# A down projection done once as seven block products instead of once per group

## Chip, cores and metric

The kernel runs on one core of a Trainium2 chip, in float32. The metric is the device time of one execution in microseconds (us), the median of the runs shown. A float32 value is carried as a pair: a high part in the format that TensorE takes (`fp32r`) and a low part, the remainder. A product of two such pairs takes three matmuls (high·high, high·low, low·high), which `mm3` issues; making the pair ("split") takes one copy on ACT (the high part) and one subtraction on DVE (the low part).

## What is computed

One layer over 1024 tokens of width 1024: a half-step feed-forward, a mixer of convolution and state space, a second half-step feed-forward, a final norm. The change lies in the second feed-forward, whose inner width is 2816 (22 tiles of 128).

```python
def swiglu(h, w_gate, w_up, w_down):
    return (jax.nn.silu(h @ w_gate) * (h @ w_up)) @ w_down
...
h = modulate(rms_norm(x, ffn2_norm[l]), sh3, sc3)
x = x + 0.5 * g3[:, None, :] * swiglu(h, ffn2_w_gate[l], ffn2_w_up[l], ffn2_w_down[l])
return rms_norm(x, final_norm)
```

## The kernel before

Everything is transposed: features lie on partitions and tokens along a row, in two halves of 512 (`h` is 0 or 1). `x[k][h]` is tile k of the residual. The Python program is written in one order, and a scheduler then sets each engine's order; each engine runs its own list strictly in order. DMAs are all issued by SP, in the order of its list.

The feed-forward works in eleven groups of two inner tiles (`fi` 0 and 1). Group 0 (`group0`, tiles named `fb0`) takes the gate and up projections tile by tile with `proj`, eight `mm3` for each tile and half of the tokens. Groups 1 to 10 (`seven`, tiles `fb1` to `fb10`) take each of the two projections as a 2 by 2 block product by a scheme of seven block products instead of eight: left operands are blocks of the normalised input (`A11`, `A12`, `A22` and the sums `S1` to `S4`, made once by `combos` and named `h3S`), right operands are blocks of the weights and their sums, which POOL makes in `Weights.combine` (lines 158 to 160) into the tile `sums`. One side, gate or up, is 7 products of 4 `mm3`, so a group is 14 x 12 = 168 matmuls. They accumulate in three PSUM banks per side, of the pool `mm_ps` with six.

After a group's products, `down2` multiplies its two activation tiles with its rows of the down weights: 8 output tiles, 2 halves and 2 inner tiles make 32 `mm3`, 96 matmuls of 512 columns, and DVE adds each of the 16 results to `x` (scaled by `gate`). This is called from `between` inside the next group's `seven`, behind the product number `place`: 0 in group 1, which puts `fb0d` between the first and the second product of `fb1`, and 1 in the others. The last two groups' down projections are done together behind group 10 (`fb10d`, a loop at the end of the kernel), the last quarter of it in two pieces of 256 columns; `after2` squares each finished `x` tile for the final norm, and `Sumsq.rstd` sends the sums (`n4..st`), the root on DVE and the spreading (`n4..bc`) to PE and DVE some `mm3` later.

Weights come through `Weights`: a source array of 1 MB is loaded into one of two buffers of `rawp` (`raw`), in `granules` of two chunks of 512 columns it is split by ACT and DVE into a tile `w`, and `w` has three slots here (`ringp`), each free again when PE has done with it. A granule of `seven` serves two products, 24 matmuls. The split activations live in the pool `movA` (20 tiles of 4 KB per partition) and `movB` (12), `x` in a pool of its own.

In the profile's names, `x` tiles are `x`, split activations of a group `fb_0a` and `fb_1a`, the final norm's `n4_0_0` appears as `n_0`. Line 101 is the helper that issues the instructions of PE, ACT, DVE and SP.

Of the kernel before, what the change touches and what calls it, by code (L numbers as in the profile page):

```python
# [34 lines left out]
SEVEN_FROM = (6, 1)  # L35
J = S // TAU
# [74 lines left out]
class Weights:  # L111
# [56 lines left out]
    def pump(self):  # L168
        while self.slots and len(self.tiles) < len(self.granules):
            i = len(self.tiles)  # L170
            pair = self.granules[i]
            (j0, c0), (j1, c1) = pair
# [9 lines left out]
            if j0 == j1 and isinstance(c0, int) and c1 == c0 + 1:  # L182
# [34 lines left out]
def hymba_layer(ctx: ExitStack, tc, x_d, wm1_d, wmod_d, gu1_d, gs1_d, wd1_d, win_d, wout_d, glu_d, gu2_d, gs2_d, wd2_d, cols_d, cond_d, lam_d, bc_d, out_d):  # L217
# [13 lines left out]
    xp = pool("xp", side="right")  # L231
# [3 lines left out]
    movs = {"A": pool("movA", bufs=20)}  # L235
# [57 lines left out]
    stream(gu2_d, gs2_d, wd2_d, SEVEN_FROM[1])  # L293
# [219 lines left out]
    def seven(name, between, place=1):  # L513

        a_tiles, gate_, taken = {}, {}, []
        for side in "gu":
# [5 lines left out]
            def out(h, fi, t):  # L522
                nm = f"{name}_{fi}_{h}"
# [3 lines left out]
                else:  # L527
                    V.tensor_tensor(out=t[:], in0=t[:], in1=gate_[h, fi][:], op=ALU.mult)
                    a_tiles[fi, h] = split_act(t[:], nm + "a")

            for n, (left, b) in enumerate(SEVEN):
# [39 lines left out]
                if side == "g" and n == place:  # L571
                    between()
        return a_tiles

    def down2(a_tiles, n, name, halves=(1, 0)):
        wd = ws.take(2)
        for dh in range(2):
# [7 lines left out]
            ws.free()  # L585

# [716 lines left out]
    movs["B"] = ctx.enter_context(tc.tile_pool(name="movB", bufs=12))  # L1303
# [14 lines left out]
    ctx.callback(sums_open.close)  # L1318

    def group0():  # L1320

        a_tiles, pg, pu = {}, {}, {}
        g0, u0, g1 = ws.take(3)
        ready(act3, 0, KT)
        pg[0, 0], pu[0, 0] = proj(g0, act3[0], "fb0g0_0"), proj(u0, act3[0], "fb0u0_0")
        gu_evac(0, 0, pg[0, 0], pu[0, 0], a_tiles, "fb0_0_0")
        pg[1, 0] = proj(g1, act3[0], "fb0g1_0")
        ready(act3, 1, KT)
        pg[0, 1] = proj(g0, act3[1], "fb0g0_1")
# [7 lines left out]
        for h in range(2):  # L1337
            gu_evac(1, h, pg[1, h], proj(u1, act3[h], f"fb0u1_{h}"), a_tiles, f"fb0_1_{h}")
        ws.free()
        return a_tiles  # L1340

    clock.side.append(combos(act3, "h3", "BAAA"))
    a_prev = group0()
    blocks["free"] = True
    a_prev = seven("fb1", lambda: down2(a_prev, 2, "fb0", (0, 1)), 0)
    for g in range(2, NGRP - 1):
        a_prev = seven(f"fb{g}", lambda: down2(a_prev, 2, f"fb{g - 1}"))
    a_last, a_prev = a_prev, seven("fb10", lambda: None)
    n4 = {}
    WHOLE = [slice(0, HALF)]  # L1350
    PIECES = (WHOLE, [slice(0, HALF // 2), slice(HALF // 2, HALF)])

    def after2(d, h, tok):
        n = tok.stop - tok.start
        if d == 0:
            n4[h, tok.start] = Sumsq(f"n4_{h}_{tok.start}", n, acc_in_mov)
        ss = n4[h, tok.start]
        ss.add(x[d][h][:, tok], apart=d == KT - 1, beside=d < 6)

        def use(bc):  # L1360
            for k in range(KT):
                xs = x[k][h][:, tok]
# [88 lines left out]
```

## Time and profile before

| | |
|---|---|
| runs | 1801.97, 1801.79, 1800.12 us; median 1801.79 |
| profiled execution, span from first to last instruction | 1799.7 us |
| around the span (the three runs less the span) | 0.4 to 2.3 us; 2.1 for the median |
| matmuls, as the profile counts them | 7772 |
| busy shares | PE 96%, DVE 67%, ACT 27%, POOL 12% |
| granted TensorE clock | 0.989 of full |
| moved by DMA | 165 MB, 92 GB/s over the span |

The profile lists one execution, by its span; the time of that execution itself is not listed, so that it is taken as the span and the 2.1 us that the median lies above it. Busy time of PE counts a matmul to the end of its pipeline: the mean of one is 389 ns where one starts every 227 ns. Rates are therefore taken from starts. In the list of waits and in the timeline, what stands behind an arrow is what released the instruction.

The second feed-forward runs from 1105 us to the end.

### The profile page before, as it was taken

Reading aid. Unit: us, or ns where it says so; the run is one execution under the profiler, and the core shown is the slowest. Engines: PE = TensorE matmul, PEld = TensorE weight load, DVE = VectorE, ACT = ScalarE, POOL = GpSimd, SP = SyncE. Lnnn points to the kernel's source line nnn. Section 1 sums busy time; section 2 is a strip of 40 time slices with the busy share of each in tenths; the row PEclk is TensorE's granted clock in tenths of the full one; section 3 lists DMA queues with packets and bytes.
Section 4 is the critical chain, followed back from the end, with each engine's and each line's share of the span. In section 5 each row is a group of like instructions: output and inputs, shape, how many; then the busy total and the mean of one; then the engine's idle time right before and its main releaser. Section 6 shows DMA issues by size and latency. Waiting matters only on the chain.

```text
span 1799.7 us, 20080 instructions
## 1 busy us (share of the span) xinstructions
PE 1725.3 (96%) x7772; PEld 1421.5 (79%) x7772; DVE 1210.3 (67%) x2182; ACT 490.9 (27%) x750; POOL 222.7 (12%) x143
## 2 busy tenths in 40 slices
PE   4998989999999999999999999999999999999996
PEld 3786767788788888877888888788888888888885
DVE  7999999847765566482665737975655565556546
ACT  4311212112222223342213424432222223222331
POOL 0000000001512112110000012021212111211211
PEclk9998999999999999999999999999999999999997
DMA  7625665410111111314763110111111111111102
GB/s 305 232 72 181 208 207 203 162 48 24 47 47 50 61 54 48 111 48 119 221 200 98 48 47 24 47 48 47 62 56 47 48 65 52 47 49 66 50 24 94
DMA packets 58737, 165.02 MB, mean 92 GB/s; under 512 B 14353, under 2 KB 29969, under 8 KB 43922
## 3 DMA queue, kind: packets, MB, share of 16 engines
q1 hardware_dynamic: 58642, 163.74, 26.6%
q8 instruction: 61, 1.00, 0.2%
q14 instruction: 34, 0.28, 0.0%
HBM read 140.64 MB, written 18.87 MB: 89 GB/s over the span
## 4 chain that ended last, share of the span: by engine, by line
PE 75%; DVE 4%; DMA 1%; POOL 1%; ACT 1%; issue 0%; SPq 0%; DVEq 0%; ACTq 0%; POOLq 0%
PE wo L101 5%; PE b L101 2%; PE v L101 2%; PE c L101 2%; PE fb10d L101 2%; PE fa10d L101 2%; PE u L101 1%; PE fb0u L101 1%; PE fa5u L101 1%; PE fb8d L101 1%; PE fb7d L101 1%; PE fb6d L101 1%; PE fb5d L101 1%; PE fb4d L101 1%; PE fb3d L101 1%; PE fb2d L101 1%
## 5 line engine op out<-in xcount | busy, mean ns | idle before, releaser
L101 ACT CAST w<-raw 128x1024 fp32r<-128x1024 f32 (+1 forms) x203 | 171.6, 861 | 516.0 <-POOL raw L159 58.0
L101 DVE TENSOR_TENSOR w<-raw,w 128x1024 fp32r<-128x1024 f32 (+1 forms) x203 | 208.4, 1040 | 77.8 <-ACT w L101 75.6
L158 POOL TENSOR_TENSOR sums<-raw 128x1024 f32<-128x1024 f32 x30 | 77.5, 2582 | 1119.8 <-DVE w L101 668.8
L101 DVE TENSOR_TENSOR w<-sums,w 128x512 fp32r<-128x512 f32 x90 | 59.7, 689 | 47.0 <-ACT w L101 46.6
L101 ACT CAST w<-sums 128x512 fp32r<-128x512 f32 x90 | 52.8, 619 | 133.3 <-PE fa6d L101 9.7
L101 DVE CUSTOM_DVE_ANT_0 wm<-wm,cact 128x1024 f32<-128x1024 f32 x48 | 57.7, 1212 | 0.0
L101 PE MATMUL wo<-oa,w 128*128 128x512 f32 x192 | 45.4, 391 | 0.6 <-DVE w L101 0.6
L101 PE MATMUL u<-h,w 128*128 128x512 f32 x192 | 44.9, 392 | 0.8 <-DVE w L101 0.8
L101 PE MATMUL v<-h,w 128*128 128x512 f32 x192 | 45.4, 393 | 0.0
L101 PE MATMUL c<-h,w 128*128 128x512 f32 x192 | 45.2, 392 | 0.0
L101 PE MATMUL wo<-ob,w 128*128 128x512 f32 x192 | 45.2, 391 | 0.0
L101 PE MATMUL b<-h,w 128*128 128x512 f32 x192 | 44.9, 392 | 0.0
L101 PEld LDWEIGHTS u<-h,w 128*128 128x128 f32 x192 | 35.6, 188 | 9.1 <-DVE w L101 1.2
L101 PEld LDWEIGHTS wo<-oa,w 128*128 128x128 f32 x192 | 35.8, 188 | 8.7 <-DVE w L101 1.1
L101 PEld LDWEIGHTS wo<-ob,w 128*128 128x128 f32 x192 | 35.8, 188 | 7.4
L101 PEld LDWEIGHTS b<-h,w 128*128 128x128 f32 x192 | 35.7, 188 | 7.2
L101 PE MATMUL p<-h,w 128*128 128x512 f32 x144 | 36.1, 409 | 5.4 <-DVE h L101 3.0
L101 PEld LDWEIGHTS c<-h,w 128*128 128x128 f32 x192 | 35.6, 188 | 7.1
L101 PEld LDWEIGHTS v<-h,w 128*128 128x128 f32 x192 | 35.5, 188 | 7.0
L159 POOL TENSOR_TENSOR raw<-sums,raw 128x512 f32<-128x512 f32 x30 | 40.2, 1341 | 2.4
L160 POOL TENSOR_TENSOR sums<-raw 128x512 f32<-128x512 f32 x30 | 40.1, 1338 | 2.4
L339 POOL TENSOR_TENSOR n3aq<-n3aq,n3aq 128x512 f32<-128x512 f32 x5 | 6.5, 1291 | 267.0 <-ACT n3aq L101 266.9
(1095 smaller groups left out, 4025.1 us busy)
## 6 DMA issues: line engine op xcount, KB each, us to landing
raw<-in_gs SPq DMA_DIRECT2D x30, 1024.0 KB, 4.8
wm<-in_wmod SPq DMA_DIRECT2D x24, 1024.0 KB, 5.4
raw<-in_wd SPq DMA_DIRECT2D x22, 1024.0 KB, 4.9
raw<-in_gu SPq DMA_DIRECT2D x14, 1024.0 KB, 4.9
mw<-in_wm SPq DMA_DIRECT2D x8, 1024.0 KB, 9.3
raw<-in_win SPq DMA_DIRECT2D x8, 1024.0 KB, 5.4
x<-in_x SPq DMA_DIRECT2D x8, 512.0 KB, 7.3
mw<-in_wmod SPq DMA_DIRECT2D x4, 1024.0 KB, 4.8
```

The lines of the kernel that those rows point to most:

```text
L101: r = getattr(self.engine, name)(*args, **kw)
L158: self.G.tensor_tensor(out=f[:, :1024], in0=r[:, 512:1536], in1=r[:, :1024], op=ALU.subtract)
L159: self.G.tensor_tensor(out=r[:, 512:1024], in0=f[:, 512:1024], in1=r[:, :512], op=ALU.add)
L160: self.G.tensor_tensor(out=f[:, 1024:], in0=r[:, 1536:], in1=r[:, 512:1024], op=ALU.subtract)
L339: nc.gpsimd.tensor_tensor(out=a, in0=a, in1=sq[:, :n], op=ALU.add)
```

## The change

The activations of all eleven groups are now kept and the down projection is done once behind group 10, as a 2 by 2 block product over the whole inner width of 22 tiles (`KH` = 11 in each half).

- **Groups.** The inner tiles are ordered so that group g holds tile g of the first half and tile g of the second. `seven` and `group0` write the activations, unsplit, into two tiles of a `Left` (`fb1l` and so on). In the next group's `between`, now at place 1 in all groups and without matmuls, `Left.sums` adds four block sums on DVE (`fb1s`) and SP stores all seven left operands into DRAM (`l2_d`, 1.75 MB in seven rows of 256 KB a group). `right_sums` loads the group's 1 MB of down weights (`wd_0`, `wd_1`), makes four sums on POOL and stores them (`t2_d`); group 0's down weights are handled so in `late`, near the end of group 4, and `late` of group 10 loads and splits the first left operands of the down projection.
- **Down projection** (`down7`). Seven passes, in the order of `PASSES`; each is 11 inner tiles times 4 output tiles, 44 `mm3`. Passes write by turns into four banks X and four banks Y, so that DVE reads a pass's result while PE writes the other banks; three results are accumulated on. `Lefts` loads left operands back, two tiles of 128 by 512 at a time (`fbLr`), and splits them (`fbLh`, `fbLl`) ahead of use; the right operands come through `Weights` as granules of two chunks. The last pass goes over the tokens in two pieces of 256 columns.
- **Residual.** `x` (4 MB) is stored to DRAM in group 0 (`x2_d`) and loaded back during passes 0, 1, 2 and 4 (`y`), so that its room goes to `movA` (28 tiles). `movB` has 10 and is closed behind group 10; in its place five more slots for `w` open from pass 2 on.

PE's list at the start of `fb1` (`fb1gA<-h_0` is the first product, `h3S` are the sums; a number behind a name tells buffers apart), before:

```order
L101 MATMUL fb1gA<-h_0_8289,w_8664 128x512 x3
L101 MATMUL fb1gA<-h_0_8297,w_8664 128x512 x3
L101 MATMUL fb1gA<-h_0_8318,w_8664 128x512 x3
L101 MATMUL fb1gA<-h_0_8326,w_8664 128x512 x3
L101 MATMUL fb0d_0_8818<-fb_0_0a,w_8705 128x512 x3
L101 MATMUL fb0d_0_8818<-fb_1_0a,w_8705 128x512
L101 MATMUL fb0d_0_8826<-fb_0_0a,w_8705 128x512
L101 MATMUL fb0d_0_8818<-fb_1_0a,w_8705 128x512 x2
```

and now:

```order
L107 MATMUL fb1gA<-h_0_8289,w_8666 128x512 x3
L107 MATMUL fb1gA<-h_0_8297,w_8666 128x512 x3
L107 MATMUL fb1gA<-h_0_8318,w_8666 128x512 x3
L107 MATMUL fb1gA<-h_0_8326,w_8666 128x512 x3
L107 MATMUL fb1gB<-h3S_0_8596,w_8666 128x512 x3
L107 MATMUL fb1gB<-h3S_1_8656,w_8666 128x512 x3
L107 MATMUL fb1gB<-h3S_2_8727,w_8666 128x512 x3
L107 MATMUL fb1gA<-h_0_8334,w_8707 128x512 x2
L107 MATMUL fb1gB<-h3S_3_8785,w_8666 128x512
```

The 96 matmuls of `fb0d` stood between the first and the second product; now the second product, which reads `S2`, follows at once.

DVE's list at the same place, where the last `S2` and `S3` tiles are made (`h3S_3`), before:

```order
L101 TENSOR_TENSOR w_8795<-raw_8611,w_8795 128x1024
L101 TENSOR_TENSOR h3S_3_8785<-f_3_8765,h3S_3_8785 128x512
L101 TENSOR_TENSOR fb_1_1a<-fb_1_1af,fb_1_1a 128x512
L101 TENSOR_TENSOR h3S_3_8813<-f_3_8763,h3S_3_8813 128x512
L101 SCALAR_TENSOR_TENSOR x_0_97<-fb0d_0_8818,gate,x_0_97 128x512
L101 TENSOR_TENSOR f_0_8833<-h_0_8334 128x512
L101 TENSOR_TENSOR s_0_8835<-h3S_0_8590 128x512
L101 SCALAR_TENSOR_TENSOR x_0_97<-fb0d_0_8826,gate,x_0_97 128x512
L101 SCALAR_TENSOR_TENSOR x_0_99<-fb0d_0_8838,gate,x_0_99 128x512
```

and now:

```order
L107 TENSOR_TENSOR w_8791<-sums_8662,w_8791 128x512 x2
L107 TENSOR_TENSOR h3S_3_8785<-f_3_8765,h3S_3_8785 128x512
L107 TENSOR_TENSOR h3S_3_8811<-f_3_8763,h3S_3_8811 128x512
L107 TENSOR_TENSOR f_0_8829<-h_0_8334 128x512
L107 TENSOR_TENSOR s_0_8831<-h3S_0_8596 128x512
L107 TENSOR_TENSOR fb1gu_8833<-fb1gt_8814,fb1gB 128x512
L107 TENSOR_TENSOR w_8839<-raw_8403,w_8839 128x512
L107 TENSOR_TENSOR w_8839<-raw_8617,w_8839 128x512
L107 TENSOR_TENSOR fb0s_8848<-fb0l_8416 128x512
L107 TENSOR_TENSOR fb0s_8848<-fb0l_8415,fb0l_8416 128x512
L107 TENSOR_TENSOR fb0s_8849<-fb0s_8848,fb0l_8415 128x512
```

The additions to `x` are gone, the splits of the next weights (`w`) and the sums of group 0's left operands (`fb0s`) have moved up between the `h3S` tiles, and the splits of the activations are gone.

POOL's list from the second `combine` on, before:

```order
L158 TENSOR_TENSOR sums_9003<-raw_8798 128x1024
L159 TENSOR_TENSOR raw_8798<-sums_9003,raw_8798 128x512
L160 TENSOR_TENSOR sums_9003<-raw_8798 128x512
L158 TENSOR_TENSOR sums_9148<-raw_9012 128x1024
L159 TENSOR_TENSOR raw_9012<-sums_9148,raw_9012 128x512
```

and now:

```order
L169 TENSOR_TENSOR sums_8835<-raw_8617 128x1024
L170 TENSOR_TENSOR raw_8617<-sums_8835,raw_8617 128x512
L171 TENSOR_TENSOR sums_8835<-raw_8617 128x512
L676 TENSOR_TENSOR wd_1_8857<-wd_1_8857,wd_0_8856 128x512
L677 TENSOR_TENSOR wd_0_8856<-wd_0_8856 128x512
L678 TENSOR_TENSOR wd_0_8856<-wd_1_8857,wd_0_8856 128x512
L679 TENSOR_TENSOR wd_1_8857<-wd_1_8857,wd_0_8856 128x512
L169 TENSOR_TENSOR sums_9025<-raw_8844 128x1024
L170 TENSOR_TENSOR raw_8844<-sums_9025,raw_8844 128x512
```

Four additions for the down weights (`wd`) stand between two groups' weight sums.

At the end of pass 5, DVE's list now has the last pass's splits ahead of the additions that wait for pass 5 (before, there was no such pass):

```order
L107 TENSOR_TENSOR fbLl_4_12799<-fbLr_4_12763,fbLh_4_12798 128x1024
L107 TENSOR_TENSOR fbLl_6_12811<-fbLr_6_12796,fbLh_6_12810 128x1024
L107 TENSOR_TENSOR w_12718<-raw_12620,w_12718 128x512
L107 TENSOR_TENSOR fbLl_8_12850<-fbLr_8_12808,fbLh_8_12849 128x1024
L107 TENSOR_TENSOR fbLl_10_12860<-fbLr_10_12847,fbLh_10_12859 128x512
L107 SCALAR_TENSOR_TENSOR y_0_11808<-fbDY_0_12164,gate,y_0_11808 128x512
L107 SCALAR_TENSOR_TENSOR y_0_11808<-fbDY_1_12165,gate,y_0_11808 128x512
```

The diff, cut to its core:

```diff
-    movs = {"A": pool("movA", bufs=20)}
+    movs = {"A": pool("movA", bufs=28)}
...
+KH = NF // 2
+PASSES = (("A11", "B11", "X"), ("A12", "B21", "Y"), ("S2", "T2", "X"), ("S1", "T1", "Y"), ("S3", "T3", "X"), ("S4", "B22", "Y"), ("A22", "T4", "X"))
...
+        def product(h, fi, t, other):
+            if keep is None:
+                V.tensor_tensor(out=t[:], in0=t[:], in1=other, op=ALU.mult)
+                a_tiles[fi, h] = split_act(t[:], f"{name}_{fi}_{h}a")
+            else:
+                V.tensor_tensor(out=keep.at(h, fi), in0=t[:], in1=other, op=ALU.mult)
...
+        def sums(self):
+            (a11, a12), (a22, a21) = [[t[:, i, :] for i in range(2)] for t in self.tiles]
+            self.store(0, 2, self.tiles[0][:])
+            self.store(6, 1, self.tiles[1][:, 0:1, :])
+            o, e = (mov(f"{self.name}s{i}", dtype=F32) for i in range(2))
+            V.tensor_tensor(out=o[:, 0, :], in0=a21, in1=a22, op=ALU.add)
+            V.tensor_tensor(out=o[:, 1, :], in0=a11, in1=a21, op=ALU.subtract)
+            V.tensor_tensor(out=e[:, 0, :], in0=o[:, 0, :], in1=a11, op=ALU.subtract)
+            V.tensor_tensor(out=e[:, 1, :], in0=a12, in1=e[:, 0, :], op=ALU.subtract)
+            self.store(2, 2, o[:])
+            self.store(4, 2, e[:])
+
+    def right_sums(k, wd_d, t_d):
+        lo, hi = (mov(f"wd{k}_{i}", dtype=F32) for i in range(2))
+        for i, t in enumerate((lo, hi)):
+            SP.dma_start(t[:], wd_d[2 * i : 2 * i + 2, k].rearrange("c p n -> p c n"))
+        b11, b12, b22, b21 = lo[:, 0, :], lo[:, 1, :], hi[:, 0, :], hi[:, 1, :]
+        G_.tensor_tensor(out=b22, in0=b22, in1=b12, op=ALU.subtract)
+        G_.tensor_tensor(out=b12, in0=b12, in1=b11, op=ALU.subtract)
+        G_.tensor_tensor(out=b11, in0=b22, in1=b11, op=ALU.add)
+        G_.tensor_tensor(out=b21, in0=b21, in1=b11, op=ALU.subtract)
+        for i, t in enumerate((lo, hi)):
+            SP.dma_start(t_d[2 * i : 2 * i + 2, k].rearrange("c p n -> p c n"), t[:])
...
+        def get(self, m, k):
+            i = m * ((KH + 1) // 2) + k // 2
+            if k % 2 == 0:
+                self.load(i + 4)
+                self.ahead(i + 3)
...
+    def down7(lefts, n, name, after, last_pieces, beside):
+        for m, (_, right, b) in enumerate(PASSES):
+            opens = right in ("B11", "B21", "T1")
+            if opens:
+                banks[b] = [(ps if b == "X" or i < 2 else psum_small)(f"{name}{b}{m}_{i}") for i in range(4)]
+            bank = banks[b]
+            if m < 6:
+                for k in range(KH):
+                    beside(m, k)
+                    if step % 2 == 0:
+                        (w,) = ws.take()
+                    act = lefts.get(m, k)
+                    for i in range(4):
+                        mm3(bank[i][:], w, step % 2 * 4 + i, act, opens and k == 0, k == KH - 1, more=not opens)
...
+            for tok in last_pieces:
+                for i in range(4):
+                    for k in range(KH):
+                        mm3(bank[i][:, tok], held_w[k // 2], k % 2 * 4 + i, lefts.get(m, k), False, k == KH - 1, tok, more=True)
+                    put(i, i, 1, True, tok)
...
-    a_prev = seven("fb1", lambda: down2(a_prev, 2, "fb0", (0, 1)), 0)
-    for g in range(2, NGRP - 1):
-        a_prev = seven(f"fb{g}", lambda: down2(a_prev, 2, f"fb{g - 1}"))
-    a_last, a_prev = a_prev, seven("fb10", lambda: None)
+    for g in range(1, NGRP):
+        this = Left(l2_d, g, f"fb{g}")
+        def between(g=g, before=left):
+            before.sums()
+            right_sums(g, wd2_d, t2_d)
...
+        seven(f"fb{g}", between, 1, this, late)
+        left = this
...
+    down7(lefts, 2, "fbD", after2, PIECES[1], beside)
```

`put(i, d, h, done, tok)` adds a bank to `x[d][h]` on DVE and calls `after2` when that tile is done.

229 lines of the change are left out of this document (172 added, 57 removed).

## The prediction

> **What bounds the kernel now.** I read the busy times, then the chain of work, then busy times by stretch with the chain's pieces beside them.
>
> ```profile
> PE 1725.3 (96%) x7772; PEld 1421.5 (79%) x7772; DVE 1210.3 (67%) x2182; ACT 490.9 (27%) x750; POOL 222.7 (12%) x143
> PE 75%; DVE 4%; DMA 1%; POOL 1%; ACT 1%; issue 0%; SPq 0%; DVEq 0%; ACTq 0%; POOLq 0%
> ...
> 1278.42 21.76 PE fb2d L101 x96
> ...
> core 0: us, PE busy (x) PEld busy (x) DVE busy (x) ACT busy (x) POOL busy (x), PEclk, DMA share, GB/s
> 1150.43:1212.98 62.55, 61.22 (x265) 49.09 (x264) 52.53 (x77) 21.97 (x36) 11.00 (x6) 1.00 0.15 51
> 1212.98:1729.78 516.80, 516.80 (x2281) 428.07 (x2280) 302.41 (x424) 139.72 (x223) 89.15 (x51) 1.00 0.15 53
> 1729.78:1785.70 55.92, 50.86 (x277) 44.21 (x275) 31.08 (x68) 13.45 (x26) 13.66 (x15) 0.95 0.10 42
> ```
>
> A group's down projection is 96 matmuls in 21.76 us, so a matmul of 512 columns costs 226.67 ns. The long stretch (groups 2 to 10, down projections 1 to 8) is 2280 of them: 516.8 us, the whole stretch. PE there waits for nothing, and a matmul removed is 226.67 ns gained. In the first stretch (`fb1` and `fb0d`, 264 matmuls, 59.84 us) 2.7 us are lost, and DVE is busy 52.5 of 62.6 us: the one place where DVE is close to being the bound. The last is `fb10d`, below.
>
> **Matmuls removed.** Eleven groups of 96 before; seven passes of 132 now: 1056 against 924. 256 columns cost more than half of 512, so pieces are counted apart:
>
> ```profile
> 1774.14 2.94 PEld L101 LDWEIGHTS fb10d<-fb_1a,w 128*128 128x128 f32 x24
> 1782.08 1.22 PE L101 MATMUL n_0bc<-ident,n_0rb 128*128 128x128 f32 x4 [3.49 <-DVE n_0rb L101]
> 1782.95 2.91 PE L101 MATMUL fb10d<-fb_1a,w 128*128 128x256 f32 x12
> L101 PEld LDWEIGHTS fb10d<-fb_1a,w x144: 187/192/333, 1740.9 to 1785.2; 128*128 128x128 f32 x144
> ```
>
> 24 weight loads start within 2.94 - 0.19 us: 119.7 ns each. Before: 1008 of 512 columns and 96 of 256, 228.5 + 11.5 = 240.0 us. Now: 792 and 264, 179.5 + 31.6 = 211.1 us. **-28.9 us**; its error is that of 119.7 ns, 5 ns of which would be 0.8 us.
>
> **Start of `fb1`.** `fb0d` gave PE 21.8 us of work while DVE made `S2` and `S4`. That cover goes; with it go 16 additions to `x` and some splits on DVE. Two things must be in time: the last `S2` tile, and the last `S4` tile.
>
> ```profile
> 1150.43 2.88 PE L101 MATMUL fb1gA<-h,w 128*128 128x512 f32 x12
> 1117.29 1.41 DVE L101 SCALAR_TENSOR_TENSOR h3t<-x,scl,n3bbc 128x512 f32<-128x512 f32 x2 [3.01 <-PE n3bbc L101]
> 1121.53 2.05 DVE L101 SCALAR_TENSOR_TENSOR h3t<-x,scl,n3bbc 128x512 f32<-128x512 f32 x3
> 1123.50 2.06 DVE L101 SCALAR_TENSOR_TENSOR h<-h3t,mods,h 128x512 fp32r<-128x512 f32 x3
> 1132.67 1.23 DVE L101 TENSOR_TENSOR w<-raw,w 128x1024 fp32r<-128x1024 f32 x1 [0.74 <-ACT w L101]
> 1133.82 0.68 DVE L101 TENSOR_TENSOR h3S<-f,h3S 128x512 fp32r<-128x512 f32 x1
> 1134.42 0.68 DVE L101 TENSOR_TENSOR f<-f,f 128x512 f32<-128x512 f32 x1
> 1183.96 2.40 POOL L158 TENSOR_TENSOR sums<-raw 128x1024 f32<-128x1024 f32 x1 [64.17 <-DVE w L101]
> 1184.34 4.26 DVE L101 TENSOR_TENSOR w<-raw,w 128x512 fp32r<-128x512 f32 x2
> 1183.96:1189.75 5.79, 5.64 (x25) 4.17 (x24) 5.79 (x5) 1.14 (x2) 5.63 (x3) 1.00 0.26 74
> ```
>
> From start to start DVE takes 0.66 us for a product with a constant (three from 1121.53 to 1123.50), 1.15 us for a split of 1024 and 0.605 us for an operation of 512. Nothing ahead of 1117.29 differs on DVE. From there the new list has 61 operations up to the last `S2` tile: 16 x 0.66 + 2 x 1.15 + 43 x 0.605 = 38.9 us, done at 1156.2. PE reaches it after 23 matmuls of `fb1`, at 1150.43 + 5.2 = 1155.6. But POOL's second weight sum now starts at about 1155.5, when the weight split just ahead frees `sums`; at 1184 two DVE operations that met it took 4.26 instead of 1.3 us, and the three operations of that sum cost DVE 5.79 us for 5 operations, 2.8 us too long. So I take a wait of 2.5 us (0.6 without POOL). From there to the last `S4` tile DVE has 32 operations, 19.4 us, and what is left of that sum and the four `wd` additions hold it up by another 3.6 us: 1158.2 + 23.0 = 1181.2. PE's list has 120 matmuls (27.2 us) ahead of it, so it comes at 1150.4 + 27.2 + 2.5 = 1180.1 and waits 1.1, with the smaller ones 1.5 us. In all 4.0 us for 2.7 before: **+1.3 us**. Bounds: no wait, -2.7; all of POOL's time here (5.6 us for the sum, as much again for the four additions) on PE, +8.5.
>
> [...]
>
> **Groups 2 to 10.** What is added must hide under 168 matmuls, 38.1 us, where 264, 59.8 us, were.
>
> ```profile
> 1278.42:1338.26 59.84, 59.84 (x266) 49.57 (x265) 35.07 (x49) 15.76 (x25) 10.34 (x6) 1.00 0.14 52
> L101 DVE SCALAR_TENSOR_TENSOR x<-fb2d,gate,x 128x512 f32<-128x512 f32 x16 | 12.0, 750 | 7.4 <-PE fb2d L101 7.3
> L101 DVE TENSOR_TENSOR w<-raw,w 128x1024 fp32r<-128x1024 f32 x22 | 27.8, 1262 | 9.3 <-ACT w L101 8.4
> L101 DVE TENSOR_TENSOR w<-sums,w 128x512 fp32r<-128x512 f32 x51 | 33.8, 689 | 25.5 <-ACT w L101 25.4
> L158 POOL TENSOR_TENSOR sums<-raw 128x1024 f32<-128x1024 f32 x17 | 44.4, 2610 | 405.5 <-DVE w L101 405.5
> L159 POOL TENSOR_TENSOR raw<-sums,raw 128x512 f32<-128x512 f32 x17 | 22.5, 1321 | 1.3
> raw<-in_gs SPq DMA_DIRECT2D x30, 1024.0 KB, 4.8
> ```
>
> DVE: 35.1 less 12.0 (additions to `x`), 2 x 1.26 (splits of down weights) and 4 x 0.69 (splits of activations), plus 4 x 0.69 (left sums): 20.6 of 38.1 us. POOL: 10.3 + 4 x 1.32 = 15.6 us. A slot of `w` falls free two granules, 10.9 us, before its next content is used; ACT and DVE need some 2.5 us for it. The tightest is the first granule of the next group: `sums` is free when the last granule is split, 24 us into the group; POOL's first two operations take 3.9 us, the split 2.3, so it stands at 31 of 38. POOL's `wd` additions wait for loads that stand in SP's list behind the stores of the left sums; these sums are made at the group's start, and a store and a load one behind the other take 10 us at 4.8 each, so the additions (5.3 us) end some 16 us into the group, and POOL is wanted only at 24. I cost all this at **0**; the cover is these 7 us. Bounds 0 to one POOL operation a group, 9 x 2.6 = 23 us.
>
> **Passes 0 to 5.** A granule is 24 matmuls, 5.44 us. In this DVE splits 1024 columns of weights and 1024 of left operand, 2 x 1.26, ACT the same at 1.05; at a pass's end four additions, 3.0 us, with left operands split two pairs ahead, 10.9 us. Banks change over a whole pass, 29.9 us. The transfers are 44.6 MB (77 right and 77 left blocks of 256 KB, 4 MB of `x`) in 219 us: 204 GB/s.
>
> ```profile
> 850.00:1000.00 150.00, 149.25 (x767) 127.02 (x766) 95.92 (x174) 37.36 (x56) 0.00 (x0) 1.00 0.53 163
> 0.00:45.00 45.00, 20.70 (x69) 15.48 (x70) 31.72 (x63) 19.54 (x23) 0.70 (x6) 0.96 0.79 305
> x<-in_x SPq DMA_DIRECT2D x8, 512.0 KB, 7.3
> mi<-mi_d SPq DMA_DIRECT2D x8, 256.0 KB, 2.8
> ```
>
> 163 GB/s took 0.53 of the DMA engines, with PE busy 149 of 150 us; 204 would take 0.66, and 305 have been seen. A load of 1 MB may be sent two granules of work before its split. **0**; bounds 0 to the rival below.
>
> **The end.** `fb10d` took 55.92 us; 144 x 226.67 and 96 x 119.7 ns are 44.1. The other 11.8 us are the final norm's small matmuls and PE's waits for them, 3.49 us the longest; behind it 12 matmuls took 2.91 us, 0.24 each, twice the usual. Now the last pass has 33 matmuls for an output tile instead of 12, which spaces these steps out. Small matmuls stay, 4.9 us. The first sum waits for DVE, ACT and POOL to finish pass 5's squares (2.9 us behind pass 5, with 14 matmuls, 1.7 us, ahead of it): 1.2. The two roots (some 3 us of DVE's small operations against 22 and 21 matmuls): 0.9 and 0.6. With 0.4 at the start, 8.0 us: **-3.8 us**. Bounds -6.9 (no waits) and +4 (the long wait and slow matmuls twice). That DVE's splits stand ahead of its additions at the end of pass 5 keeps the last pass's operands out of this. Behind the last matmul all is as it was: 0.
>
> **Sum.** -28.9 + 1.3 - 3.8 = -31.4 us. The span goes from 1799.7 to 1768.3, and with the 2.1 us that the median lies above it the time is 1770.4 us.
>
> **Rivals.**
> - [...] At `fb1` all 11.2 us of POOL fall on PE's path: +8.5 instead of +1.3, and 1777.6. For it: the 2.56 us-long operations at 1184. Against: DVE got through 5 operations in that sum's time. [...]
> - *Each group waits for its first granule* by one POOL operation, since POOL, SP and DVE now share 38 us instead of 60: +23, 1794. It would turn the change into a loss from 31.4 / 9 = 3.5 us a group. Against it: the 7 us of cover.
> - *Slower: the passes are bound by transfers.* One SP list carries right operands (two buffers of 1 MB), left operands and `x`. If each landed before the next, 4.8 + 2 x 7.3 = 19.4 us stand against 10.9 us of matmuls for each 2 MB, 19 times: +163 us, 1933. With 256 KB at 2.8 us as the measure it is 4.8 + 4 x 2.8 = 16, +98. It is slower than before from 12.5 us per 2 MB on, 178 GB/s. Against it: transfers overlapped at 305 GB/s.
>
> **How the numbers follow.** The forecast, 1764 to 1776, gets 0.66; the port 0.13 (1776 to 1782); waiting groups 0.09 (1782 to 1798); transfers 0.07, of which 0.06 end slower; better than 1764 0.03; the rest, 0.02, is no change. The range 1764 to 1783 holds a little over 0.8. 0.2% (3.6 us) is about what a measurement of this kernel can tell from no change: faster 0.92, same 0.02, slower 0.06.
>
> **What would show it.** Right: 924 matmuls under `fbD`, groups 2 to 10 at 38.1 us each, six passes at 29.9 us, waits of about 4 us of PE in `fb1` for `h3S`, a last pass of about 39 us, nothing in PE's waits on `fbLl` or `w` in the passes. Wrong: PE waiting for `w` in each group (POOL or SP), for `fbL` or `w` in the passes with a DMA behind it, or 512-column matmuls that no longer take 226.67 ns.

## The result and the profile after

The changed kernel takes 1780.67 us (median of 4 runs, 1779.35 to 1781.46), the kernel before 1800.95 us beside it (4 runs): a ratio of 0.9889, 95% interval 0.9875 to 0.9903. It is faster, by 20.3 us where 31.4 were forecast. The time lies inside the range of 1764 to 1783 us, but above the forecast's own part of it (1764 to 1776, with a chance of 0.66): it fell into the part given to the rival in which all of POOL's time in `fb1` falls on PE's path (1776 to 1782, 0.13; in the chances, "the port"). Its profiled execution spans 1779.3 us. One of the four executions of e9 below took 3826 us, and e9's median and ratio are those of the other three.

The busy times and the chain of work, from the page of the changed kernel:

```profile
PE 1703.8 (96%) x7724; PEld 1407.8 (79%) x7724; DVE 1214.9 (68%) x2109; ACT 520.4 (29%) x765; POOL 302.9 (17%) x187
PE 74%; DVE 3%; POOL 1%; DMA 1%; ACT 1%; issue 1%; SPq 0%; DVEq 0%; ACTq 0%; POOLq 0%
```

POOL has 44 operations more, as announced, and is busy 80 us longer, where 44 at the forecast's 1.32 us are 58. The busy times by stretch (`fb1`; groups 2 to 10; passes 0 to 5; last pass; behind the last large matmul; columns as in the prediction's table):

```profile
1150.90:1205.30 54.40, 43.97 (x171) 34.68 (x170) 43.41 (x56) 15.62 (x27) 17.65 (x10) 0.91 0.32 116
1205.30:1548.00 342.70, 342.70 (x1513) 283.87 (x1512) 219.84 (x279) 105.10 (x173) 155.96 (x91) 1.00 0.48 169
1548.00:1727.50 179.50, 179.50 (x793) 148.70 (x792) 109.34 (x107) 79.19 (x90) 15.05 (x10) 1.00 0.67 235
1727.50:1766.70 39.20, 37.74 (x301) 37.30 (x300) 19.00 (x54) 4.54 (x10) 5.26 (x6) 0.96 0.21 81
1766.70:1779.30 12.60, 2.32 (x14) 1.88 (x12) 5.94 (x22) 0.42 (x1) 0.00 (x0) 0.69 0.24 83
```

All but the first are within 1.5 us of the forecast. Groups 2 to 10 take 1512 x 226.67 ns = 342.7 us and the six passes 792 x 226.67 ns = 179.5 us, to the hundredth: PE waits for nothing, with the DMA engines 0.67 busy at 235 GB/s. (The 0.66 at 204 GB/s of the forecast were a mean over all seven passes; over these it is 0.58 at 207 GB/s.) The last pass takes 39.2 us (39 forecast). `fb1` takes 54.3 us for 168 matmuls, 38.1 us: 16.2 us are lost there, 4.0 were forecast. PE's waits in it (us in total, times, longest):

```profile
PE fb1gC L107 <- ACT h3S L107: 4.0, 1, 4.0
PE fb1gB L107 <- DVE fb1gu L107: 3.9, 1, 3.9
PE fb1uB L107 <- DVE fb1uu L107: 2.5, 1, 2.5
```

and as they stand on PE's timeline (start, length, count, and in brackets the idle time ahead):

```profile
1163.96 4.58 PE L107 MATMUL fb1gB<-h3S,w 128*128 128x512 f32 x12 [3.92 <-DVE fb1gu L107]
1168.38 2.23 PE L107 MATMUL fb1gC<-h3S,w 128*128 128x512 f32 x9
...
1183.82 0.50 PE L107 MATMUL fb1gC<-h3S,w 128*128 128x512 f32 x1 [4.03 <-ACT h3S L107]
...
1190.80 2.88 PE L107 MATMUL fb1uB<-h3S,w 128*128 128x512 f32 x12
...
1198.20 4.51 PE L107 MATMUL fb1uB<-h,w 128*128 128x512 f32 x12 [2.48 <-DVE fb1uu L107]
1202.55 2.90 PE L107 MATMUL fb1uC<-h3S,w 128*128 128x512 f32 x12
```

The waits are 10.4 us. Behind each of them PE is slow for a while: 12 matmuls from 1163.96 to 1168.38 take 4.42 us instead of 2.72 (granted clock 0.62, and 0.50 over the first 2.44 us of it), the 23 from 1183.82 to 1190.80 6.98 instead of 5.21 (0.76, and 0.50 from 1184.80 to 1186.93), 12 from 1198.20 4.35 (0.62, and 0.50 over the first 3.20 us). This time at half clock is another 5.1 us, and 15.5 of the 16.2 us are found. In the experiments half clock stands for what the matmuls behind a wait take above 226.67 ns each; what brings it, and what ends it, is not shown.

DVE's and POOL's timelines, and one row of ACT, show who was late. DVE first:

```profile
1156.48 3.49 DVE L107 TENSOR_TENSOR h3S<-f,h3S 128x512 fp32r<-128x512 f32 x2
1159.89 1.74 DVE L107 TENSOR_TENSOR f<-h 128x512 f32<-128x512 f32 x1
1161.56 1.74 DVE L107 TENSOR_TENSOR s<-h3S 128x512 f32<-128x512 f32 x1
1163.23 0.68 DVE L107 TENSOR_TENSOR fb1gu<-fb1gt,fb1gB 128x512 f32<-128x512 f32 x1
...
1176.31 1.78 DVE L107 TENSOR_TENSOR s<-h3S 128x512 f32<-128x512 f32 x1
1178.01 3.44 DVE L107 TENSOR_TENSOR w<-sums,w 128x512 fp32r<-128x512 f32 x2
1181.38 1.74 DVE L107 TENSOR_TENSOR f<-f,s 128x512 f32<-128x512 f32 x1
1183.05 0.68 DVE L107 TENSOR_TENSOR f<-h 128x512 f32<-128x512 f32 x1
...
1196.13 1.33 DVE L107 TENSOR_TENSOR w<-raw,w 128x1024 fp32r<-128x1024 f32 x1 [4.13 <-ACT w L107]
1197.38 0.67 DVE L107 TENSOR_TENSOR fb1uu<-fb1ut,fb1uB 128x512 f32<-128x512 f32 x1
```

```profile
1156.69 2.72 POOL L169 TENSOR_TENSOR sums<-raw 128x1024 f32<-128x1024 f32 x1 [36.40 <-DVE w L107]
1159.50 1.59 POOL L170 TENSOR_TENSOR raw<-sums,raw 128x512 f32<-128x512 f32 x1
...
1175.94 1.61 POOL L676 TENSOR_TENSOR wd<-wd,wd 128x512 f32<-128x512 f32 x1 [13.18 <-DMA wd<-in_wd]
...
1190.87 2.78 POOL L169 TENSOR_TENSOR sums<-raw 128x1024 f32<-128x1024 f32 x1 [8.30 <-DVE w L107]
...
1195.05 1.56 ACT L107 CAST w<-raw 128x1024 fp32r<-128x1024 f32 x2 [3.92 <-POOL raw L170]
```

- The first wait is for a bank, not for an operand. `S3`'s product accumulates on bank B, and may not start until DVE has read `S2`'s result there (`fb1gu<-fb1gt,fb1gB` at 1163.23). That reading stands in DVE's list behind four operations that met POOL's weight sum: from 1156.48 to 1163.23 they take 6.75 us, where four take 2.4 (0.60 from start to start).
- The second is for `S4`'s last tile but one, behind four DVE operations that met POOL's `wd` additions: 6.74 us from 1176.31 to 1183.05, again for 2.4. In all POOL took 8.7 us from DVE.
- The third is a bank again: DVE's `fb1uu` stands behind a weight split that waits for ACT and, through it, for POOL's sum from 1190.87 on. Here POOL is waited for; it does not hold DVE up.

My theory was: DVE is late in `fb1` because POOL's operations hold it up there, and its list, kept strictly in order, passes each delay on to the readings of banks that PE waits for. The rival: DVE's own list is too long for `fb1` without `fb0d`'s matmuls over it, and POOL matters little.

### The profile page after: what moved, and what is told of

Read it like the earlier page. It is cut to its first block, busy times and chain, and to the rows that moved or that the text cites. A ratio compares the mean times of both kernels' runs of the same rounds, so it can differ in the third digit from the quotient of the medians.

```text
span 1779.3 us, 20370 instructions
## 1 busy us (share of the span) xinstructions
PE 1703.8 (96%) x7724; PEld 1407.8 (79%) x7724; DVE 1214.9 (68%) x2109; ACT 520.4 (29%) x765; POOL 302.9 (17%) x187
## 4 chain that ended last, share of the span: by engine, by line
PE 74%; DVE 3%; POOL 1%; DMA 1%; ACT 1%; issue 1%; SPq 0%; DVEq 0%; ACTq 0%; POOLq 0%
PE fbDX L107 7%; PE fbDY L107 5%; PE wo L107 5%; PE b L107 2%; PE v L107 2%; PE c L107 2%; PE fa10d L107 2%; PE u L107 1%; PE fb0u L107 1%; PE fa5u L107 1%; PE fb0g L107 1%; PE fa8d L107 1%; PE fa7d L107 1%; PE fa6d L107 1%; PE fa4d L107 1%; PE fa4u L107 1%
## 5 line engine op out<-in xcount | busy, mean ns | idle before, releaser
L107 DVE TENSOR_TENSOR w<-raw,w 128x1024 fp32r<-128x1024 f32 (+1 forms) x220 | 256.6, 1179 | 123.2 <-ACT w L107 122.1
L169 POOL TENSOR_TENSOR sums<-raw 128x1024 f32<-128x1024 f32 x30 | 80.7, 2689 | 846.8 <-PE fa5u L107 436.7
L107 PE MATMUL fbDX<-fbLh,w 128*128 128x512 f32 (+1 forms) x440 | 115.4, 349 | 0.0
L107 PEld LDWEIGHTS fbDX<-fbLh,w 128*128 128x128 f32 x440 | 78.0, 191 | 10.4
L107 PE MATMUL fbDY<-fbLh,w 128*128 128x512 f32 x264 | 81.8, 389 | 0.0
L107 PE MATMUL fbDX<-fbLl,w 128*128 128x512 f32 (+1 forms) x220 | 76.7, 349 | 0.0
L107 DVE TENSOR_TENSOR fbLl<-fbLr,fbLh 128x1024 fp32r<-128x1024 f32 (+1 forms) x42 | 48.9, 1172 | 15.8 <-ACT fbLh L107 14.5
L107 PEld LDWEIGHTS fbDY<-fbLh,w 128*128 128x128 f32 x264 | 49.6, 188 | 10.3
L107 PE MATMUL fbDY<-fbLl,w 128*128 128x512 f32 x132 | 51.3, 389 | 0.0
L107 PEld LDWEIGHTS fbDX<-fbLl,w 128*128 128x128 f32 x220 | 42.1, 191 | 5.1
L107 PE MATMUL wo<-oa,w 128*128 128x512 f32 x192 | 45.4, 391 | 0.6 <-DVE w L107 0.6
L107 ACT CAST fbLh<-fbLr 128x1024 fp32r<-128x1024 f32 (+1 forms) x42 | 40.5, 976 | 18.6 <-DMA fbLr<-l_d 18.0
L107 PE MATMUL v<-h,w 128*128 128x512 f32 x192 | 45.4, 393 | 0.0
```

Source lines behind the costliest of these rows:

```text
L107: r = getattr(self.engine, name)(*args, **kw)
L169: self.G.tensor_tensor(out=f[:, :1024], in0=r[:, 512:1536], in1=r[:, :1024], op=ALU.subtract)
```

## The experiments

Single profiles start `fb1` anywhere from 1147.4 to 1152.8 us, and what stands from pass 0 on differs by up to 2.7 us, whatever the experiment. Stages are therefore compared by the time from the first matmul of `fb1g` to the first of `fb3g` (336 matmuls, 76.2 us without a wait), and the medians stand beside it. Each stage time is that of one profile, which need not be a median execution (e1's is the fastest of four, 1770.46 to 1775.58 us), and what half clock costs behind a wait differs between profiles (0.1 to 2.6 us): a gain by the stage and the same gain by the median differ by up to 3.6 us, so that smaller differences rest on the rows shown. All ratios are to the kernel before on the same chip, whose median was 1800.2 to 1801.3 us.

| kernel | `fb1` + `fb2`, us | median, us | ratio, 95% interval |
|---|---|---|---|
| changed kernel | 92.4 | 1780.67 | 0.9875 to 0.9903 |
| e1 `wd` of group 1 late | 84.9 | 1774.44 | 0.9833 to 0.9864 |
| e2 and no second weight sum | 80.7 | 1769.68 | 0.9812 to 0.9841 |
| e3 left sums of `fb0` late | 87.5 | 1774.23 | 0.9839 to 0.9872 |
| e4 ACT copies bank B | 89.7 | 1780.50 | 0.9865 to 0.9902 |
| e5 `wd` loads first | 88.7 | 1777.44 | 0.9855 to 0.9888 |
| e6 e1, and ACT copies bank B | 83.4 | 1768.29 | 0.9808 to 0.9837 |
| e8 both sides' plain products first; `wd` and left sums late | 83.4 | 1773.52 | 0.9838 to 0.9867 |
| e9 group 1 plain; `wd` late | 81.6 (360 matmuls) | 1769.62 | 0.9813 to 0.9846 |
| e10 e8, two `sums` | 84.5 | 1776.35 | 0.9852 to 0.9879 |
| e11 e1, second sum on DVE | 81.4 | 1770.19 | 0.9820 to 0.9846 |
| e12 e8, second sum on DVE | 80.5 | 1766.83 | 0.9804 to 0.9831 |
| e13 e12, third sum on DVE too | 76.6 | 1765.74 | 0.9791 to 0.9819 |

### POOL's operations taken away

e1 moves the `wd` additions:

```diff
-            right_sums(g, wd2_d, t2_d)
+            if g > 1:
+                right_sums(g, wd2_d, t2_d)
...
-            if g == 4:
-                right_sums(0, wd2_d, t2_d)
+            if g in (4, 6):
+                right_sums(g // 2 - 2, wd2_d, t2_d)
```

> Group 1's loads, the four wd additions on POOL and the stores are made in group 6 instead of in fb1; nothing is left out. Theory (POOL holds DVE up): in fb1 the DVE operations that met these additions took 1.74 us instead of 0.68, 4.4 us in all, and the last S4 tile was waited for 4.0 us. Without them that wait goes: 1780.7 - 4.0 = 1776.7 us, DVE's operations between S3 and S4 are back at 0.6 to 0.7 us, and group 6 still costs 38.1 us. Rival (DVE's own list is too long once fb0d's matmuls do not cover it; POOL matters little): the wait stays, 1780 to 1781.

e2 adds to e1 that the second weight source of `fb1` takes the sums of the first, so that three operations of POOL are left out:

```diff
+        self.reuse = 11
...
     def combine(self, j):
...
         r = self.raws[j]
+        if len(self.sums) == self.reuse:
+            self.sums[j] = self.sums[j - 1]
+            return
```

> As e1, and the second weight source of fb1 uses the sums of the first, so that three more POOL operations are left out of fb1 (the output is not the reference's). Theory (POOL holds DVE up): DVE gets back 4.3 us ahead of its reading of bank B as well, the wait of 3.9 us for bank B goes, and with it the 1.65 us of half clock behind it: 1776.7 - 3.9 - 1.65 = 1771.1 us; a wait of 2 to 3 us late in fb1, for fb1uu, stays. Rival (DVE's own list): 1780 to 1781, all waits stay.

PE's waits from `fb1` to `fb2`, in e1 and, below the dots, in e2:

```profile
PE fb1gB L107 <- DVE fb1gu L107: 3.9, 1, 3.9
PE fb1uB L107 <- DVE fb1uu L107: 2.5, 1, 2.5
...
PE fb1uB L107 <- DVE fb1uu L107: 2.4, 1, 2.4
```

In e1 the wait for `h3S` is gone and the other two stand as they were: 7.5 us less, since the 1.8 us of half clock behind it went too, and 1.5 behind the third, which the edit does not touch. In e2 the wait for `fb1gu` goes as well: both stages take 11.6 us less than in the changed kernel, and of PE's waits only the third is left (2.4 us, with 1.7 us of half clock behind it, 1.3 of it in the first 12 matmuls). DVE has 87 operations in the two stages in all three kernels; the rival gave 1780 to 1781 us for both and falls. The seven of POOL's ten operations in `fb1` that e2 takes out of it cost 11.6 us.

### DVE's work, and SP's order

e3 moves the left sums, e5 swaps two lines.

```diff
+            if g > 1:
+                before.sums()
-            before.sums()
             right_sums(g, wd2_d, t2_d)
...
-        def late(g=g):
+        def late(g=g, before=left):
+            if g == 1:
+                before.sums()
```

> fb0's left sums (two stores, four DVE additions, two stores) are made late in fb1's up side instead of early in its gate side; nothing is left out. They take DVE 4 x 0.6 = 2.4 us between the first wait and the second. Theory (separate waits, each with its own last cause): behind them DVE waited 1.57 us for PE's A22 product anyway, so little of it reaches S4: 0 to -1.0 us, 1779.7 to 1780.7. Rival (DVE's throughput bounds fb1 as a whole, whatever the operation): -2.4 us, 1778.3.

```diff
+            if g == 1:
+                right_sums(g, wd2_d, t2_d)
             before.sums()
-            right_sums(g, wd2_d, t2_d)
+            if g > 1:
+                right_sums(g, wd2_d, t2_d)
```

> In fb1 alone right_sums(1) is written ahead of fb0's left sums, so that its two loads stand in SP's list ahead of the four stores instead of behind them; nothing is left out and every engine has the same operations. In the changed kernel these loads let POOL's four additions start only at 1175.9, among S4's tiles; with the left sums taken away (e3) they started at 1159.1. Theory (SP's order put the additions on S4's path): they move to about 1160 to 1167, the wait of 4.0 us for the last S4 tile goes, a wait of up to 2 us at bank B can come for it: fb1 takes 48 to 52 us instead of 54.3, 1774.7 to 1778.7 us. Rival (e3 gained because DVE had four operations less): fb1 stays at 54 us, 1780 to 1781.

e3 gained more than either theory said, in `fb1` alone 7.6 us, of which `fb2` gave 2.7 back. The cause is not the 2.4 us of DVE alone: with the stores of the left sums gone from SP's list, the `wd` loads behind them came sooner, and POOL's additions with them. From e3's timelines (POOL; PE in `fb2`):

```profile
1159.11 1.71 POOL L676 TENSOR_TENSOR wd<-wd,wd 128x512 f32<-128x512 f32 x1
...
1204.77 3.03 PE L107 MATMUL fb2gB<-h3S,w 128*128 128x512 f32 x12 [2.40 <-DVE fb2gu L107]
```

The 2.40 us are the left sums of two groups in a row, met by POOL. e5 tells the two apart: all engines have the same work, and only SP's order differs. Its additions start at 1164.57 instead of 1175.94, the wait for `h3S` is gone, and bank B is waited for a second time:

```profile
PE fb1gB L107 <- DVE fb1gu L107: 5.9, 2, 3.9
```

So SP's order alone is worth 3.7 us, where e3 gained 4.9 over both groups; how the rest of e3's gain divides is not shown. That the `wd` loads stand behind stores which wait for DVE was in the prediction for groups 2 to 10, where it costs nothing; in `fb1` it put POOL among `S4`'s tiles.

### Is it the bank?

e4, in `fb1` alone:

```diff
                 elif n == 1:
                     u2 = t2k(nm + "u2")
-                    add(u2, t1, "B")
+                    A.copy(u2[:], bank["B"][:])
+                    V.tensor_tensor(out=u2[:], in0=u2[:], in1=t1[:], op=ALU.add)
```

> In fb1 ACT copies bank B behind S2's product and DVE adds from the copy, so that S3's product waits for ACT instead of for DVE; nothing is left out, DVE's count is the same, ACT has two operations of 512 more. Theory: the wait of 3.9 us for bank B shrinks to 1 or 2 us, which shows that it was the bank's reuse and not an operand that PE waited for. But PE then comes earlier to S4, whose last tile DVE still makes late: that wait grows from 4.0 by what the first gave, less the 1.6 us that DVE waited for A22: 1778 to 1780 us. Rival (PE waited for S3's tiles, not for the bank): the first wait stays at 3.9 us with an h3S tile behind it, 1780 to 1781.

From e4's timelines (ACT, PE, DVE):

```profile
1158.12 0.58 ACT L107 COPY fb1gu<-fb1gB 128x512 f32<-128x512 f32 x1
...
1158.75 3.01 PE L107 MATMUL fb1gB<-h3S,w 128*128 128x512 f32 x12
...
1169.61 5.49 PE L107 MATMUL fb1gB<-h,w 128*128 128x512 f32 x12 [3.85 <-DVE fb1gu L107]
...
1168.88 0.68 DVE L107 TENSOR_TENSOR fb1gu<-fb1gt,fb1gB 128x512 f32<-128x512 f32 x1
```

`S3`'s product starts at 1158.75, with no wait: its tiles were there, and the first wait was for the bank. DVE is no earlier, and 3.85 us are lost at the next product on that bank. The two stages gained 2.7 us, which the median does not show (1780.50 us). e6 adds e1's edit and lets ACT copy the bank for the second reading too:

```diff
             def add(dst, src, b):
+                if name == "fb1" and b == "B" and dst is not src:
+                    A.copy(dst[:], bank[b][:])
+                    V.tensor_tensor(out=dst[:], in0=dst[:], in1=src[:], op=ALU.add)
+                    return
```

> e1 (the four wd additions of group 1 made in group 6), and in fb1 ACT copies bank B after its first and its second product on both sides, with DVE adding from the copy; nothing is left out. Theory: e1's fb1 of 46.8 us has 3.9 us of waiting for bank B and about 1.7 us of half clock behind it; both go, and PE then waits about 2 us for S4's last tile, which DVE cannot bring earlier: fb1 takes 43 to 44 us, some 3 to 4 us less than e1, 1770.5 us. Rival (DVE's list is the limit as a whole, and the wait only moves): fb1 stays at 46 to 47 us, 1774.

`fb1` took 45.4 us instead of the 43 to 44 expected. The third wait went with the reading too, from 2.5 us to 0.7; at the second reading PE waited 4.37 us. From e6's timelines (POOL; one of 13 DVE operations in that time; ACT; PE):

```profile
1153.55 9.93 POOL L169 TENSOR_TENSOR sums<-raw 128x1024 f32<-128x1024 f32 x1 [36.49 <-DVE w L107]
...
1159.35 0.69 DVE L107 TENSOR_TENSOR f<-f,s 128x512 f32<-128x512 f32 x1
...
1164.84 1.14 ACT L107 CAST w<-raw 128x512 fp32r<-128x512 f32 x2 [7.84 <-POOL raw L170]
...
1167.04 4.40 PE L107 MATMUL fb1gB<-h,w 128*128 128x512 f32 x12 [4.37 <-ACT fb1gu L107]
```

Here POOL is the one that is held up: its operation takes 9.93 us instead of 2.72, while DVE runs on at its usual 0.6 us from start to start; ACT waits for POOL, and the copy of the bank stands behind that in ACT's list. So "DVE is late" is half of it: DVE or POOL, whichever loses, has PE behind it.

### Cover

e9 takes two groups plainly:

```diff
-SEVEN_FROM = (6, 1)
+SEVEN_FROM = (6, 2)
...
-    left = group0()
+    left = before = plain_group(0)
     blocks["free"] = True
+    left = plain_group(1)
...
-    for g in range(1, NGRP):
+    for g in range(2, NGRP):
```

> Group 1 is taken plainly like group 0 (192 matmuls instead of 168), the first seven-product group is group 2, and S4's tiles are made during group 1; right_sums of groups 0 and 1 are made in groups 4 and 6; nothing is left out. It costs 24 matmuls, 5.4 us, and gives DVE 43.5 us of cover, twice what fb0d gave. Theory (what is lost in fb1 is lost for want of cover): fb1 takes 43.5 us, fb2 38.1 to 39 us: 10 to 11 us less than the changed kernel, 1770 us. Rival (the waits come from what POOL and DVE have to do at the first seven-product group wherever it stands): they appear in fb2, and the kernel takes 1780.7 + 5.4 = 1786 us.

```profile
1149.13:1192.65 43.52, 43.52 (x193) 36.04 (x192) 28.08 (x38) 10.92 (x17) 6.02 (x3) 1.00 0.21 78
1192.65:1230.73 38.08, 38.08 (x169) 31.53 (x168) 25.60 (x31) 11.38 (x19) 17.23 (x10) 1.00 0.45 160
```

Both groups run at 226.67 ns a matmul: the waits do not move to `fb2`, they are gone, for 24 matmuls (5.4 us) more; 10.8 us are won, as expected. But a plain group has no weight sums either, and e9 moves the `wd` additions as e1 does, so that POOL has three operations in the first stretch instead of ten. The ten in `fb2` meet a DVE that has no `h3S` tiles left to make, and cost PE nothing. So most of the loss needs both, POOL's operations and DVE's `h3S` tiles in one stretch without `fb0d`'s cover: e2 takes away the first, e9 parts the two. The next kernel looks for cover without more matmuls: the products of `A11` and `A12` of both sides come first.

```diff
+BOTH = [(s, n) for n in (0, 2) for s in "gu"] + [(s, n) for s in "gu" for n in (1, 3, 4, 5, 6)]
...
+            if g == m:
+                pairs = [(j + (s == "u"), Weights.SEVEN[n]) for s, n in BOTH]
...
-        for side in "gu":
-            for n, (left, b) in enumerate(SEVEN):
+        order = BOTH if name == "fb1" else [(s, n) for s in "gu" for n in range(7)]
+        for q, (side, n) in enumerate(order):
+            left, b = SEVEN[n]
```

> fb1 starts with the products that need no sums, A11 and A12 of the gate and of the up side (48 matmuls, 10.9 us, instead of 24 mixed with S2's), then S2 to S4 of the one and of the other; its weight granules stand in that order. The wd additions of group 1 are made in group 6 and fb0's left sums in group 2; nothing is left out, and the matmuls are as many. Theory: the cover that fb0d gave is half restored for nothing, so neither S3's bank nor S4's last tile is waited for by more than 1 us: fb1 takes 38.1 to 42 us, 12 to 16 us less than the 54.3 of the changed kernel, 1765 to 1769 us. Rival (DVE's list up to S4 is the limit, and PE comes to the last S4 tile after about 124 matmuls in either order): a wait of 3 to 5 us there, fb1 44 to 46 us, 1771 to 1773.

The rival's size (`fb1` 45.3 us), but not its place: 3.61 us were waited for bank B at `S3`, 1.2 at `S4`. Against e1's two groups (84.9 us) the new order and the later left sums brought 1.5 us. From e8's timelines (ACT, DVE, PE):

```profile
1167.55 0.62 ACT L108 CAST w<-raw 128x512 fp32r<-128x512 f32 x1 [3.92 <-POOL raw L171]
...
1168.20 1.21 DVE L108 TENSOR_TENSOR w<-raw,w 128x512 fp32r<-128x512 f32 x1 [1.82 <-ACT w L108]
...
1170.65 4.61 PE L108 MATMUL fb1gB<-h3S,w 128*128 128x512 f32 x12 [3.61 <-DVE fb1gu L108]
```

In the new order the fifth granule needs POOL's second sum at once, and DVE's split of it stands ahead of the reading of the bank. Two ways out were tried: a second buffer for `sums` (e10), and the sum on DVE (e12; e11 is the same on top of e1).

```diff
-tc.tile_pool(name="sums", bufs=1)
+tc.tile_pool(name="sums", bufs=2 if late_sums else 1)
...
-tc.tile_pool(name="movB", bufs=10)
+tc.tile_pool(name="movB", bufs=8)
```

> As e8 (A11 and A12 of both sides first, wd additions of group 1 in group 6, fb0's left sums in group 2), with two buffers for the weight sums instead of one in the second feed-forward, so that POOL's second sum of fb1 need not wait until the first sum has been split; nothing is left out. Theory: e8's wait of 3.6 us for bank B is a chain from sums' one buffer over POOL (7.6 us), ACT's cast and DVE's split of the fifth granule to DVE's reading of the bank behind that split; with the sum made earlier it goes, with 1.7 us of half clock: fb1 takes 38.1 to 41 us for e8's 45.3, 1767 to 1769 us. Rival (POOL's time falls on DVE wherever it lies, since DVE works without a pause from fb0 on): 43 to 45 us, 1772 to 1773.

> As e1 (wd additions of group 1 in group 6), and the second weight sum of fb1 is made by DVE instead of POOL, written behind DVE's first reading of bank B; nothing is left out. [...] The wait of 3.9 us and its half clock go, fb1 takes 42.5 to 44.5 us for e1's 46.8, 1770 to 1772 us. Rival (DVE has no time to spare in fb1; giving it more work makes it later): fb1 47 to 49 us, 1775 to 1777.

> As e8, and the second weight sum of fb1 is made by DVE instead of POOL; nothing is left out. Theory: with 10.9 us of matmuls ahead of S2 and no POOL operation from fb0 to S4, DVE reads bank B in time; what may be left is a wait of 1 to 2 us for S4's last tile: fb1 takes 38.1 to 41 us, 1767 to 1769 us. Rival (the 2.4 us more on DVE come out at S4): a wait of 3 us there, fb1 42 to 43 us, 1770.

```diff
+        G = self.V if len(self.sums) == 11 else self.G
-        self.G.tensor_tensor(out=f[:, :1024], in0=r[:, 512:1536], in1=r[:, :1024], op=ALU.subtract)
+        G.tensor_tensor(out=f[:, :1024], in0=r[:, 512:1536], in1=r[:, :1024], op=ALU.subtract)
...
```

e10 went by its rival, and a little worse. The second sum came early, at 1140.4, and cost DVE 3.4 us there (three operations in 5.2 us); the third now came at 1172.4, among `S4`'s tiles, and PE waited 3.07 us for DVE's reading of bank C behind it. From e10's timelines (POOL, DVE, PE):

```profile
1172.40 2.41 POOL L170 TENSOR_TENSOR sums<-raw 128x1024 f32<-128x1024 f32 x1 [25.37 <-DMA raw<-in_gs]
...
1173.00 4.05 DVE L108 TENSOR_TENSOR w<-sums,w 128x512 fp32r<-128x512 f32 x2
...
1179.46 3.20 PE L108 MATMUL fb1gC<-h3S,w 128*128 128x512 f32 x9 [3.07 <-DVE fb1gu L108]
```

It also lost 2.3 us in groups 3 to 10, which had been free of waits; whether by the second `sums` or the smaller `movB` is not shown. e11 and e12 went by the theory that POOL's sum costs DVE more (4.35 us in the changed kernel) than the same sum on DVE (1.2 + 0.6 + 0.6 = 2.4 us, an estimate from DVE's rows): more work for DVE made it earlier. e11 took 3.5 us off e1's two groups, with DVE busy 60.6 us for 90 operations instead of 63.1 for 87, e12 2.9 off e8's. In e12 one wait of 2.07 us was left, where POOL's third sum met `S4`; e13 moves that sum to DVE as well:

```diff
-        G = self.V if len(self.sums) == 11 else self.G
+        G = self.V if len(self.sums) in (11, 12) else self.G
```

> As e12, and the first weight sum of fb2, which POOL began among S4's last tiles (2.86 and 1.00 us for two DVE operations of 0.69 us, and a wait of 2.07 us of PE with half clock behind it), is made by DVE as well; nothing is left out. Theory: DVE spends 2.4 us on it where the meeting cost it 2.5 us, but the first of its operations is written ahead of S4's last split, the others behind it; PE waits less than 1 us for S4, fb1 and fb2 together take 76.2 to 78.5 us (e12: 80.5; 336 matmuls without a wait: 76.2), 1763 to 1765 us. Rival (work on DVE is no cheaper than meeting POOL): 80 to 82 us together, 1766 to 1768.

Both groups of e13 in one stretch:

```profile
1149.29:1225.85 76.56, 76.56 (x337) 62.93 (x336) 60.96 (x91) 27.50 (x46) 16.82 (x10) 1.00 0.31 114
```

PE does not wait once in them; DVE is busy 6.4 us less than in the changed kernel though it has four operations more. At 1765.74 us (1763.27 to 1768.28) this version beats both: its interval, 0.9791 to 0.9819, lies below that of the changed kernel, 0.9875 to 0.9903. Of the 16.2 us that `fb1` lost the two stages give back 15.8, the median 14.9.

## Why the prediction was right and wrong

- **Matmuls removed**: right. 1512, 792 and 264 matmuls took 342.7, 179.5 and, in the last pass, 31.6 us by the same 119.7 ns.
- **Groups 2 to 10** and **Passes 0 to 5**, each costed at 0: right, to 0.1 us. In a group POOL was busy 17.3 us instead of the 15.6 forecast and DVE 24.4 instead of 20.6; PE waited for nothing all the same. The rivals of waiting groups and of passes bound by transfers fall with it.
- **The end**, -3.8: the last pass lost 7.6 us beyond its large matmuls instead of 11.8 (8.0 forecast), -4.2; behind the last matmul another 1.4 us went, where 0 was forecast. That the last pass came so near is in part luck: the first sum's wait was as forecast (1.3 us for 1.2) and the roots' waits of 1.5 us hardly came (0.1), but the granted clock was 0.86 over the first 12.5 us, a loss of some 1.7 us that the sum does not have.
- **Start of `fb1`**, +1.3: this is the step that failed. 16.2 us were lost there instead of 4.0, so the term is +13.5, beyond its upper bound of +8.5. With 0.6 us of later start the spans agree: -28.9 + 13.5 - 4.2 - 1.4 + 0.6 = -20.4.

The failed step asked for the last tiles of `S2` and `S4` alone. `S2`'s was in time, 2.5 us had been given to it. Four things went into it wrongly or not at all, and they act on each other, so that they do not add up. The first is that PE also waits for DVE to read a bank before the next product accumulates on it, and these readings stand in DVE's list behind the sums (e4: the wait moves with the reading); it is the first and the third wait, 6.4 us. The second is POOL's price: 5.6 us of DVE's time forecast, 8.7 measured. The forecast's own place at 1184 had shown more than was read from it. The window taken there ends within the last split; these are the rows behind the 4.26 us (kernel before):

```profile
1188.52 0.67 DVE L101 TENSOR_TENSOR fb1gu<-fb1gt,fb1gB 128x512 f32<-128x512 f32 x1
1189.12 1.78 DVE L101 TENSOR_TENSOR w<-raw,w 128x512 fp32r<-128x512 f32 x2
1190.83 0.68 DVE L101 TENSOR_TENSOR fb1gu<-fb1gu,fb1gC 128x512 f32<-128x512 f32 x1
```

From 1184.34 to 1190.83 five operations take 6.49 us where five take 3.0, so that the sum cost 3.5 us and not 2.8; in the changed kernel it was 4.35. The third is SP's order: the forecast counted the `wd` additions into the way to `S4` wherever they fall, and SP brought them right before `S4`'s last tiles (e5). The last is the half clock behind each wait, 5.1 us.

The rival that puts all of POOL's time in `fb1` on PE's path was right in what it blamed, and its 1777.6 us were nearer than the forecast: e2 shows that seven of POOL's operations in `fb1` are worth 11.6 us, and e13 that 15.8 us go with the order of the products, the place of the additions and the engine of two sums. PE's waits, 10.4 us, stayed below the 11.2 us of POOL that it allowed; it was too low since it let POOL's time itself be the worst that could fall on PE, without the 5.1 us of half clock. No run shows the port that the chances name; what the runs show is that operations of POOL and DVE that meet get longer (DVE's 1.67 us from start to start instead of 0.60, POOL's 9.93 us instead of 2.72).

## What to carry over

Where a stretch of matmuls is taken away, list for the engine that worked under it not only the operands that PE needs next but each reading that frees a PSUM bank, in that engine's own order; PE waits for the later of the two (in `fb1` 3.92 us for a bank, 4.03 us for an operand). In most cases here a wait of 2.1 to 4 us cost another 1.5 to 2.6 us of half clock, so short waits are dearer than they look. On a critical DVE a sum moved to POOL is no help: here a POOL operation of 512 that DVE met cost DVE 1.07 us, and the same operation on DVE 0.60.

## What had not been expected of the hardware

- DVE and POOL, both adding float32, took turns in the changed kernel: from 1159.5 to 1162.8 one operation of each started every 1.67 us (DVE's alone 0.60, POOL's alone 1.36, as at 1193.73 and 1195.09). But the turns are not sure: in e6 one POOL operation stood for 9.93 us, where it took 2.72 in the changed kernel, while 13 of DVE's passed at 0.60 us from start to start, and ended 2.24 us behind the last of them. In both places a DVE operation had started first, by 0.21 us at 1156.48 and by 0.22 in e6, and POOL got its turn in the one and not in the other; what decides between the two, and through what the engines hold each other up, no run here shows.
- The same wait does not always cost the same time. Behind 3.92 us idle 12 matmuls took 4.42 us in the changed kernel (granted clock 0.62) and 5.29 in e3, instead of 2.72. Behind 2.47 us idle in e1 12 matmuls took 2.85 us, behind 2.48 us in the changed kernel the same 12 took 4.35 (granted clock 0.62). In e12 the time was lost behind 2.07 us idle, and only 1.6 us after PE had gone on (10 matmuls took 3.87 us instead of 2.27, from 1179.98 to 1183.85).
